# The scaled key of the RWKV units, turned by block transfers and VectorE in place of TensorE identity products

## The chip, the cores and the metric

One core of a Trainium2 chip runs the kernel. The metric is the device time of one execution in microseconds (us), as the median of the runs shown. The profile is of one execution.

## The reference

One layer of a decoder trunk is computed for a prompt of 1024 rows and for eight samples of eight rows (1088 rows in all), in fp32. What matters here is the RWKV branch, a state of 64x64 per head that each row updates:

```python
def wkv7_scan(state0, r, decay, k, v, kk, a):
    def step(S, inp):
        r_t, w_t, k_t, v_t, kk_t, a_t = inp
        sa = jnp.einsum("bhvk,bhk->bhv", S, -kk_t)
        S = (S * w_t[:, :, None, :]
             + sa[..., None] * (kk_t * a_t)[:, :, None, :]
             + v_t[..., None] * k_t[:, :, None, :])
        y = jnp.einsum("bhvk,bhk->bhv", S, r_t)
        return S, y
...
def trunk(x, c, shift0, pool0, wkv0, pos0, W):
...
        h = rms_norm(x, lp["norm_mix"]) * (1 + sc) + sh
        P = h @ lp["w_in"]
        pr, pp, pg = jnp.split(P, [RWKV_COLS, RWKV_COLS + POOL_WIDTH], axis=-1)
        o_r, s_shift, s_wkv, v_first = rwkv7_branch(pr, shift0[l], wkv0[l], v_first, lp)
        o_p, s_pool = pool_branch(pp, pool0[l], pos0, lp)
        g_r, g_p = jnp.split(jax.nn.sigmoid(pg), 2, axis=-1)
        merged = g_r * (o_r @ lp["w_br_rwkv"]) + g_p * (o_p @ lp["w_br_pool"])
        x = x + gt * (merged @ lp["w_out"])
...
        x = x + gt * (jnp.square(jax.nn.relu(h @ lp["w_ff1"])) @ lp["w_ff2"])
```

There are eight heads of 64 channels, and 1088 x 1024 rows go through the big products (`w_in`, `w_br`, `w_out`, `w_ff1`, `w_ff2`).

## The kernel before

Features lie on the partitions and rows in the free dimension. A fp32 weight is split into a high part (ScalarE, `whi`) and a low part (VectorE, `wlo`), and each big product is three matmuls (`mm3`): high by high, high by low, low by high.

There are two phases. In **phase 1** the big products of `w_in` and of half of `w_br` make one long **stream** on TensorE (jobs with `mm` banks; the last eight, `op_job`, multiply the pooling branch). Between the stream's matmuls stand the many small products of the RWKV branch. **Phase 2** follows with `or_job` (the RWKV half of `w_br`), `w_out` and the MLP; the first `or_job` needs the RWKV branch complete: its last quarter of the contraction reads the tile pair `hx` that `post(3)` writes.

The RWKV branch is worked off in four pairs of heads (`f` = 0 to 3), one after the other in `heads`. For each, `front` makes the scaled tensors and `scores` runs three **units**: u = 0 and u = 1 are the prompt's chunks 0 to 7 and 8 to 15 (a chunk is 64 rows), u = 2 the samples. In the order u = 0, 2, 1, each unit multiplies `bk` by `ra` and masks the result into `ab`, `at` and `ad` (VectorE and ScalarE). `ra` holds the scaled receptance in `[..., 0, :]` and the scaled, negated key in `[..., 1, :]`. Then `inverse`, `level`, `affine` and the serial `chain` (the state `S`, step by step) follow, and `post` normalizes and gates. In `affine`, `first` uses `at`, whose half `at[:, :, 0, :]` is the scaled key with rows and channels of each 64x64 block exchanged and the two heads' partition halves swapped. The prompt units of before get it by sixteen fp32 products with the identity into a PSUM bank `w`, which VectorE copies. The values `v` are turned in another way already: `swap` exchanges the 32x32 blocks of each 64x64 block by four transfers on SP's queue, from DRAM into `uv`, and VectorE transposes within the 32x32 blocks.

What sets the order: TensorE executes in the order in which a planner (`Clocks`, `Pace`) emits the program; it models when operands are ready and puts a small product between stream matmuls where it expects no wait. A request of `need` says for what a generator waits. The other engines' queues are put in order by a scheduler. All queues run in order. Everything is recorded through a helper, so most lines read L187 (VectorE, ScalarE, GpSimd, SyncE) or L358 (TensorE); rows are told apart by their tiles.

Of the kernel before, what the change touches and what calls it, by code (L numbers as in the profile page):

```python
# [9 lines left out]
F32 = mybir.dt.float32  # L10
# [8 lines left out]
P = 128  # L19
D = 1024  # L20
NPR = 1024
NSEQ = 8
TS = 8
NT = NPR + NSEQ * TS
# [297 lines left out]
class K:  # L322
# [565 lines left out]
    def ra(self, d, u):  # L888

        nc, kk, r, ev, es = self.nc, d["kk"], d["r"], d["ev"], d["es"]  # L890
        C = 8 if u < 2 else 1
        cs = slice(8 * u, 8 * u + C)
        ra = self.p1.tile([P, C, 2, 64], F32, tag=f"ra{C}", bufs=2 if u < 2 else 1, name=self.nm("ra"))
        d["qs"][u] = dict(ra=ra)
        if u < 2:
            nc.vector.scalar_tensor_tensor(ra[:, :, 1, :], cut(kk[:, :NPR])[:, cs], -1.0, ev[:, cs, 0:64], op0=ALU.mult, op1=ALU.mult)
            nc.vector.tensor_tensor(ra[:, :, 0, :], cut(r[:, :NPR])[:, cs], ev[:, cs, 1:65], op=ALU.mult)
        else:
            nc.vector.scalar_tensor_tensor(cut8(ra[:, 0, 1, :]), cut8(kk[:, NPR:NT]), -1.0, es[:, :, 0:8], op0=ALU.mult, op1=ALU.mult)
            nc.vector.tensor_tensor(cut8(ra[:, 0, 0, :]), cut8(r[:, NPR:NT]), es[:, :, 1:9], op=ALU.mult)  # L900
# [18 lines left out]
    def unit(self, f, d, u):  # L919
        nc = self.nc  # L920
        bk, end, v, ad, ao = (d[k] for k in ("bk", "end", "v", "ad", "ao"))
        ident = self.kc("ident")
        prompt = u < 2
        c0, C = 8 * u, 8 if prompt else 1
        cs = slice(c0, c0 + C)
        if u == 1 and f:
            yield lambda: ("c", f - 1, 1) in self.done
        if u:
            self.ra(d, u)
        tl = lambda tag, shape, n=2: self.p1.tile([P, C] + shape, F32, tag=f"{tag}{C}", bufs=n if prompt else 1, name=self.nm(tag))  # L930
        Q = dict(ab=tl("ab", [2, 128]), uv=tl("uv", [2, 64]), ra=d["qs"][u]["ra"])
        d["qs"][u] = Q
        ra, ab, uv = Q["ra"], Q["ab"], Q["uv"]
        if prompt:
            at = Q["at"] = tl("at", [2, 64])
            ak = at[:, :, 1, :]
            rest = [uv[hs, :, 1 - h, :] for h, hs in enumerate(HB)]
            for h, hs in enumerate(HB):
                self.swap(rest[h], cut(self.d_x[8 + f][hs, c0 * 64:(c0 + C) * 64]))
            strict, incl = self.kc("strict"), self.kc("incl")  # L940
        else:
            strict, incl = self.kc("strict8"), self.kc("incl8")
            ak = Q["ak"] = tl("ak", [64])
        for a in range(0, C, 4):
            m = min(4, C - a)
            us = slice(a, a + m)
            cu = slice(c0 + a, c0 + a + m)
            yield self.need(bk[:, cu], ra[:, us], banks=("w", "w"))
            pss = [self.ps("w") for _ in HB]
            for i in range(m):  # L950
                for hs, ps in zip(HB, pss):
                    self.mm(ps[:, i * 128:(i + 1) * 128], bk[hs, c0 + a + i, :, :].rearrange("p s j -> p (s j)"),
                            ra[hs, a + i, :, :].rearrange("p s j -> p (s j)"), start=True, stop=True)
            for h, (hs, ps) in enumerate(zip(HB, pss)):
                os = HB[1 - h]
                pv = ps[:, :m * 128].rearrange("p (c s j) -> p c s j", s=2, j=64)
                nc.vector.tensor_tensor(ab[:, us, h, 0:64], pv[:, :, 0, :], incl.unsqueeze(1).to_broadcast([P, m, 64]), op=ALU.mult)
                nc.vector.tensor_tensor(ak[hs, us, :], pv[hs, :, 1, :], strict[hs].unsqueeze(1).to_broadcast([64, m, 64]), op=ALU.mult)
                for b in range(2):
                    rq = slice(os.start + 32 * b, os.start + 32 * b + 32)  # L960
                    src = pv[rq, :, 1, 32 * b:32 * b + 32]
                    if prompt:
                        nc.scalar.activation(ad[rq, cu, :], src, AF.Copy)
                        if b == 0:
                            nc.scalar.activation(ao[rq, cu, :], pv[rq, :, 1, 32:64], AF.Copy)
                    else:
                        nc.vector.tensor_tensor(ad[rq, 16, :], src[:, 0, :], strict[rq, 32 * b:32 * b + 32], op=ALU.mult)
        bh = bk[:, cs, :, :].rearrange("p c s j -> p c (s j)")
        if prompt:
            nc.vector.tensor_tensor(bh, bh, end[:, cs].unsqueeze(2).to_broadcast([P, C, 128]), op=ALU.mult)  # L970
        else:
            for s in range(2):
                nc.vector.tensor_tensor(cut8(bk[:, 16, s, :]), cut8(bk[:, 16, s, :]), end[:, 16:24].unsqueeze(2).to_broadcast([P, 8, 8]), op=ALU.mult)

        if prompt:
            for h, hs in enumerate(HB):
                nc.vector.transpose(uv[hs, :, h, :], rest[h])
        yield self.need(ra, *[] if prompt else [v[:, NPR:NT]])
        ps = self.ps("w")
        for i in range(C):  # L980
            for h, hs in enumerate(HB):
                os = HB[1 - h]
                if prompt:
                    self.mm(ps[os, i * 64:(i + 1) * 64], ra[hs, i, 1, :], ident[hs, hs], start=True, stop=True, tile_position=(hs.start, os.start))
                else:
                    self.mm(ps[hs, 0:64], v[hs, NPR:NT], ident[hs, hs], start=True, stop=True)
        if prompt:
            nc.vector.tensor_copy(at[:, :, 0, :], cut(ps))
        else:
            for h, hs in enumerate(HB):  # L990
                nc.scalar.activation(uv[hs, 0, h, :], ps[hs, 0:64], AF.Copy)
        for a in range(0, C, 4):
            m = min(4, C - a)
            yield self.need(bh[:, a:a + m], wait=0, spare=900, slack=600)
            ps = self.ps("w")
            for i in range(m):
                self.tr(ps[:, i * 128:(i + 1) * 128], bh[:, a + i, :], ident)
            nc.scalar.activation(ab[:, a:a + m, :, 64:128], ps[:, :m * 128].rearrange("p (c h j) -> p c h j", h=2, j=64), AF.Copy)
        if prompt:
            yield self.need(ak, uv)  # L1000
            ps = self.ps("w")
            for i in range(C):
                for h, hs in enumerate(HB):
                    os = HB[1 - h]
                    self.mm(ps[os, i * 64:(i + 1) * 64], ak[hs, i, :], uv[hs, i, h, :], start=True, stop=True, tile_position=(hs.start, os.start))
            nc.scalar.activation(at[:, :, 1, :], cut(ps), AF.Copy)
# [90 lines left out]
    def affine(self, f, d):  # L1097
# [4 lines left out]
        def first(u):  # L1102
            Q = d["qs"][u]
            uv, at = Q["uv"], Q["at"]
            pss = [self.ps("w") for _ in range(2)]
            for i in range(8):
                for os in HB[::-1]:
                    self.mm(pss[i // 4][os, i % 4 * 128:(i % 4 + 1) * 128], z[os, 8 * u + i, :], at[os, i, :, :].rearrange("p s j -> p (s j)"),
                            start=True, stop=True)
            for a, ps in enumerate(pss):  # L1110
                us = slice(4 * a, 4 * a + 4)
                pv = ps.rearrange("p (c s j) -> p c s j", s=2, j=64)
                nc.scalar.activation(at[:, us, 0, :], pv[:, :, 0, :], AF.Copy)
                nc.vector.tensor_copy(uv[HB[1], us, 0, :], pv[HB[1], :, 1, :])
                nc.scalar.activation(uv[HB[0], us, 1, :], pv[HB[0], :, 1, :], AF.Copy)
# [972 lines left out]
def cut(t):  # L2088
    return t.rearrange("p (c j) -> p c j", j=64)
# [6 lines left out]
def cut8(t):  # L2096
    return t.rearrange("p (c j) -> p c j", j=8)


HB = (slice(0, 64), slice(64, 128))  # L2100
# [79 lines left out]
```

## Time and profile before

| | |
|---|---|
| time, median of 2 runs | 1602.77 us (1601.74 to 1603.8) |
| the profiled execution | 1604.23 us, its span 1602.4 us |
| TensorE (PE) busy | 1544.8 us, 96% of the span |
| VectorE (DVE) busy | 1097.8 us, 69% |
| ScalarE (ACT) busy | 662.7 us, 41% |
| DMA, mean | 181 GB/s, 37920 of 137438 packets under 512 B |

PE is a matmul's busy time, PEld its weight load, SPq the queue of transfers that SyncE issues. Times in a timeline are microseconds from the span's start; the first number of a row is its start, the second how long its group lasted. A bracket tells how long the engine was idle before and what released it. A fp32 matmul appears as two instructions, so sixteen products are 32 of them.

### The profile page before, as it was taken

Reading aid. Unit: us, or ns where it says so; the run is one execution under the profiler, and the core shown is the slowest. Engines: PE = TensorE matmul, PEld = TensorE weight load, DVE = VectorE, ACT = ScalarE, POOL = GpSimd, SP = SyncE. Lnnn points to the kernel's source line nnn. Section 1 sums busy time; section 2 is a strip of 40 time slices with the busy share of each in tenths; the row PEclk is TensorE's granted clock in tenths of the full one; section 3 lists DMA queues with packets and bytes.
Section 4 is the critical chain, followed back from the end, with each engine's and each line's share of the span. In section 5 each row is a group of like instructions: output and inputs, shape, how many; then the busy total and the mean of one; then the engine's idle time right before and its main releaser. Section 6 shows DMA issues by size and latency. Waiting matters only on the chain.

```text
span 1602.4 us, 34165 instructions
## 1 busy us (share of the span) xinstructions
PE 1544.8 (96%) x13851; PEld 1453.6 (91%) x13851; DVE 1097.8 (69%) x1932; ACT 662.7 (41%) x1286; POOL 139.1 (9%) x220
## 2 busy tenths in 40 slices
PE   4999999999998999999999999999999999999997
PEld 2898888988898879989998999999999999999997
DVE  4575758776876487547542697998767796666774
ACT  4454354455334544522222572222334344344651
POOL 0100100000000000012500120000000050000000
PEclk9999999999999999999999999999999999999999
DMA  9242523234333343855884555665345996664753
GB/s 343 89 134 76 181 84 112 93 127 133 101 122 104 113 125 106 322 180 186 310 295 162 183 198 170 237 212 200 139 151 213 387 365 196 213 200 142 234 192 119
DMA packets 137438, 290.32 MB, mean 181 GB/s; under 512 B 37920, under 2 KB 42016, under 8 KB 137280
## 3 DMA queue, kind: packets, MB, share of 16 engines
q1 hardware_dynamic: 129856, 266.75, 48.4%
q10 hardware_dynamic: 5360, 14.26, 2.6%
q0 software_dynamic: 2064, 7.13, 1.3%
q8 instruction: 109, 1.79, 0.5%
q14 instruction: 49, 0.40, 0.1%
HBM read 210.80 MB, written 77.28 MB: 180 GB/s over the span
## 4 chain that ended last, share of the span: by engine, by line
PE 76%; DVE 6%; DMA 4%; issue 2%; ACT 1%; SPq 1%; DVEq 0%; ACTq 0%
PE mm L358 50%; PE w L358 13%; PE wc L358 12%; DVE wt L187 1%; DVE hx L187 1%; DMA mg<-in_w_ff 1%; DMA wt<-d_x 1%; SPq L187 1%; DMA hid<-in_w_ada_mlp 1%; DVE wlo L187 1%; DMA hid<-in_w_ff 1%; PE w L389 0%; DVE hv L187 0%; ACT wt L187 0%; DMA uv<-d_x 0%
## 5 line engine op out<-in xcount | busy, mean ns | idle before, releaser
L358 PE MATMUL mm<-hx,whi 128*128 128x362 f32 (+2 forms) x2944 | 689.9, 322 | 6.4 <-ACT px L187 3.7
L358 PEld LDWEIGHTS mm<-hx,whi 128*128 128x128 f32 x2944 | 497.3, 190 | 29.2 <-issue 11.5
L358 PE MATMUL mm<-hx,wlo 128*128 128x362 f32 (+2 forms) x1472 | 463.7, 315 | 5.8 <-DVE wlo L187 5.8
L358 PEld LDWEIGHTS mm<-hx,wlo 128*128 128x128 f32 x1472 | 279.5, 190 | 6.6 <-DVE wlo L187 6.6
L358 PE MATMUL mm<-mg,whi 128*128 128x272 f32 (+2 forms) x1312 | 249.5, 289 | 0.5 <-DVE t L187 0.5
L358 PEld LDWEIGHTS mm<-mg,whi 128*128 128x128 f32 x1312 | 205.4, 188 | 5.1 <-issue 2.5
L358 PE MATMUL mm<-mg,wlo 128*128 128x272 f32 (+2 forms) x656 | 188.5, 287 | 0.0
L358 PE MATMUL wc<-hx,whi 128*128 128x272 f32 x896 | 170.4, 287 | 0.0
L358 PEld LDWEIGHTS wc<-hx,whi 128*128 128x128 f32 x896 | 140.3, 188 | 0.0
L187 ACT ACTIVATE whi<-hid 128x512 fp32r<-128x512 f32 x128 | 80.4, 630 | 144.6 <-PE mm L358 59.6
L358 PE MATMUL wc<-hx,wlo 128*128 128x272 f32 x448 | 128.9, 288 | 1.0 <-DVE wlo L187 1.0
L358 PEld LDWEIGHTS mm<-mg,wlo 128*128 128x128 f32 x656 | 123.5, 188 | 0.0
L187 DVE TENSOR_TENSOR wlo<-hid,whi 128x512 fp32r<-128x512 f32 x128 | 87.9, 688 | 48.5 <-ACT whi L187 47.9
L187 DVE TENSOR_TENSOR wlo<-wraw,whi 128x512 fp32r<-128x512 f32 x84 | 60.7, 724 | 68.1 <-ACT whi L187 64.6
L187 ACT ACTIVATE whi<-wraw 128x512 fp32r<-128x512 f32 x100 | 62.6, 627 | 94.0 <-PE mm L358 56.9
L358 PE MATMUL w<-hx,whi 128*128 128x272 f32 (+1 forms) x480 | 96.9, 296 | 0.0
L358 PEld LDWEIGHTS wc<-hx,wlo 128*128 128x128 f32 x448 | 84.2, 188 | 1.3 <-DVE wlo L187 1.2
L187 POOL TENSOR_TENSOR hx<-hx,rs 128x64 f32<-128x64 f32 x24 | 35.2, 1465 | 569.5 <-DMA mg<-in_w_ff 376.2
L358 PEld LDWEIGHTS mm<-mg,hx 128*128 128x128 f32 x576 | 72.9, 188 | 5.0 <-issue 5.0
L358 PEld LDWEIGHTS w<-hx,whi 128*128 128x128 f32 x480 | 77.0, 188 | 0.0
L358 PE MATMUL mm<-mg,hx 128*128 128x272 f32 (+2 forms) x576 | 75.5, 290 | 0.0
L187 ACT ACTIVATE px<-mm 128x362 f32<-128x362 f32 (+3 forms) x113 | 46.3, 435 | 60.7 <-PE mm L358 53.9
(275 smaller groups left out, 2312.7 us busy)
## 6 DMA issues: line engine op xcount, KB each, us to landing
t<-d_t SPq DMA_DIRECT2D x56, 544.0 KB, 4.9
hid<-in_w_ff SPq DMA_DIRECT2D x110, 256.0 KB, 3.8
d_t<-hx SPq DMA_DIRECT2D x102, 272.0 KB, 2.2
hid<-in_w_ff SPq DMA_DIRECT2D x42, 512.0 KB, 3.8
wraw<-in_w_in SPq DMA_DIRECT2D x68, 256.0 KB, 2.8
mg<-in_w_ff SPq DMA_DIRECT2D x58, 256.0 KB, 5.4
hid<-in_w_ada_mlp SPq DMA_DIRECT2D x24, 512.0 KB, 5.7
d_th<-px SPq DMA_DIRECT2D x22, 544.0 KB, 3.0
```

Of the source, the lines that this page charges most:

```text
L187: return f(*a, **kw)
L358: return self.nc.tensor.matmul(out, lhsT, rhs, **kw)
```

## The change

`ra` now also allocates the unit's tile `ab`, and as soon as the scaled key is made, `swap` asks for eight transfers (four for each head) that exchange its 32x32 blocks into `ab[..., 0, 64:128]`, a place that is free until the later turn of `bk` writes there. In the unit, VectorE then transposes within the 32x32 blocks from there into `at[:, :, 0, :]`. The sixteen identity products, their PSUM bank, VectorE's copy and the request (`need(ra)`) ahead of them are gone for the prompt's units; the samples' unit is as before.

```diff
@@ ra
         ra = self.p1.tile([P, C, 2, 64], F32, tag=f"ra{C}", bufs=2 if u < 2 else 1, name=self.nm("ra"))
-        d["qs"][u] = dict(ra=ra)
+        ab = self.p1.tile([P, C, 2, 128], F32, tag=f"ab{C}", bufs=2 if u < 2 else 1, name=self.nm("ab"))
+        d["qs"][u] = dict(ra=ra, ab=ab)
         if u < 2:
             nc.vector.scalar_tensor_tensor(ra[:, :, 1, :], cut(kk[:, :NPR])[:, cs], -1.0, ev[:, cs, 0:64], op0=ALU.mult, op1=ALU.mult)
+            for h, hs in enumerate(HB):
+                self.swap(ab[HB[1 - h], :, 0, 64:128], ra[hs, :, 1, :])
             nc.vector.tensor_tensor(ra[:, :, 0, :], cut(r[:, :NPR])[:, cs], ev[:, cs, 1:65], op=ALU.mult)
@@ unit
-        Q = dict(ab=tl("ab", [2, 128]), uv=tl("uv", [2, 64]), ra=d["qs"][u]["ra"])
-        d["qs"][u] = Q
+        Q = d["qs"][u]
+        Q["uv"] = tl("uv", [2, 64])
...
-        yield self.need(ra, *[] if prompt else [v[:, NPR:NT]])
-        ps = self.ps("w")
-        for i in range(C):
+        if prompt:
+            nc.vector.transpose(at[:, :, 0, :], ab[:, :, 0, 64:128])
+        else:
+            yield self.need(v[:, NPR:NT])
+            ps = self.ps("w")
             for h, hs in enumerate(HB):
-                os = HB[1 - h]
-                if prompt:
-                    self.mm(ps[os, i * 64:(i + 1) * 64], ra[hs, i, 1, :], ident[hs, hs], start=True, stop=True, tile_position=(hs.start, os.start))
-                else:
-                    self.mm(ps[hs, 0:64], v[hs, NPR:NT], ident[hs, hs], start=True, stop=True)
-        if prompt:
-            nc.vector.tensor_copy(at[:, :, 0, :], cut(ps))
-        else:
+                self.mm(ps[hs, 0:64], v[hs, NPR:NT], ident[hs, hs], start=True, stop=True)
             for h, hs in enumerate(HB):
                 nc.scalar.activation(uv[hs, 0, h, :], ps[hs, 0:64], AF.Copy)
```

Counted over the program, TensorE loses 128 products of 64x64, VectorE exchanges eight copies for eight transposes of 128x8x64, SP's queue gains 64 transfers of 32x8x32, and ScalarE has 17 loads of an activation table where it had 23. Since the planner places everything anew, the order of phase 1 changes on all engines; the order of phase 2 is the same.

The first place is VectorE in the front of the first pair of heads, between the first `ra` and the weights' low part that the stream needs next (`wlo_1120` before, `wlo_1127` now). Before:

```order
L187 SCALAR_TENSOR_TENSOR ds_1062<-px_925,part,d_1061 128x64
L187 STREAM_TRANSPOSE uv_1472<-uv_1472 64x8x64
L187 SCALAR_TENSOR_TENSOR ra_1468<-wt_697,e_1011 128x8x64
L187 TENSOR_TENSOR ra_1468<-wt_1009,e_1011 128x8x64
L187 SCALAR_TENSOR_TENSOR ra_1382<-wt_697,e_1011 128x64
L187 TENSOR_TENSOR ra_1382<-wt_1009,e_1011 128x64
L187 STREAM_TRANSPOSE uv_1472<-uv_1472 64x8x64
L187 TENSOR_TENSOR bk_1015<-wt_696,wt_901 64x9x64 x2
L187 SCALAR_TENSOR_TENSOR bk_1015<-wt_902,wt_901 64x9x64 x2
L187 TENSOR_TENSOR wlo_1120<-wraw_1117,whi_1119 128x512
```

The same place now:

```order
L187 SCALAR_TENSOR_TENSOR ds_1071<-px_925,part,d_1070 128x64
L187 SCALAR_TENSOR_TENSOR ra_1486<-wt_697,e_1011 128x8x64
L187 TENSOR_TENSOR ra_1486<-wt_1009,e_1011 128x8x64
L187 SCALAR_TENSOR_TENSOR ra_1422<-wt_697,e_1011 128x64
L187 TENSOR_TENSOR ra_1422<-wt_1009,e_1011 128x64
L187 STREAM_TRANSPOSE at_1236<-ab_1047 128x8x64
L187 TENSOR_TENSOR bk_1015<-wt_696,wt_901 64x9x64 x2
L187 SCALAR_TENSOR_TENSOR bk_1015<-wt_902,wt_901 64x9x64 x2
L187 TENSOR_TENSOR wlo_1127<-wraw_1124,whi_1126 128x512
```

Two transposes of `uv` and one more a few rows further up have moved behind `wlo`, and one new transpose of `ab` stands in their place.

The second place is VectorE in the last unit (u = 1) of the third pair of heads, behind `ra`. Before, the masks of the unit's products follow at once:

```order
L187 SCALAR_TENSOR_TENSOR ra_5017<-wt_4253,e_4457 128x8x64
L187 TENSOR_TENSOR ra_5017<-wt_4455,e_4457 128x8x64
L187 TENSOR_TENSOR ab_5020<-w_5052,kct 128x4x64
L187 TENSOR_TENSOR at_5022<-w_5052,kct 64x4x64
L187 TENSOR_TENSOR ab_5020<-w_5053,kct 128x4x64
```

Now the transpose of the exchanged blocks stands three rows behind `ra`, and the pooling branch's work (`d`, `psm`, `px`) lies around it:

```order
L187 SCALAR_TENSOR_TENSOR ra_5069<-wt_4317,e_4537 128x8x64
L187 TENSOR_TENSOR ra_5069<-wt_4535,e_4537 128x8x64
L187 TENSOR_TENSOR wlo_5124<-wraw_5121,whi_5123 128x512
L187 TENSOR_TENSOR d_5135<-px_4935 128x1038
L187 TENSOR_TENSOR psm_5136<-psm_4936 128x183
L187 STREAM_TRANSPOSE at_5082<-ab_5070 128x8x64
L187 TENSOR_TENSOR px_4934<-d_5135 128x1036
L187 TENSOR_TENSOR psm_5139<-psm_5136 128x181
L187 TENSOR_TENSOR ab_5070<-w_5177,kct 128x4x64
```

What moved: VectorE now waits in its queue for transfers that can only start once the row five places ahead is done.

The third place is TensorE at the end of phase 1. `post(3)` works in three pieces of the rows, each with two sums over a head (products `w<-wt,kct`: one of `y`, one of its square). Before, the very last of them stands inside the stream, with 66 stream matmuls (the rest of this `op_job` and the next) between it and the first `or_job`:

```order
L358 MATMUL mm_8260<-hx_7484,whi_8185 128x362
L358 MATMUL mm_8260<-hx_7486,whi_8185 128x362
L358 MATMUL mm_8260<-hx_7484,wlo_8186 128x362
L358 MATMUL w_8268<-wt_8144,kct 128x362
L358 MATMUL mm_8261<-hx_7484,whi_8185 128x362
L358 MATMUL mm_8261<-hx_7486,whi_8185 128x362
L358 MATMUL mm_8261<-hx_7484,wlo_8186 128x362
```

Now the last stream matmul of phase 1 (`mm_8208`) comes ahead of the last three sums, and the first `or_job` (`mm_8333`) directly behind them:

```order
L358 MATMUL mm_8208<-hx_7188,whi_8087 128x362
L358 MATMUL mm_8208<-hx_7190,whi_8087 128x362
L358 MATMUL mm_8208<-hx_7188,wlo_8088 128x362
L358 MATMUL w_8258<-wt_8184,kct 128x362
L358 MATMUL w_8267<-wt_7132,kct 128x362
L358 MATMUL w_8275<-wt_8184,kct 128x362
L358 MATMUL mm_8333<-hx_7192,whi_8304 128x364
```

VectorE's rows behind the middle one of these sums (`w_8267`, of the third piece's `y`) are now, up to the low half of `hx` that the first `or_job` reads in its last quarter:

```order
L187 SCALAR_TENSOR_TENSOR wt_7132<-w_8267,wt_7132 128x362
L187 RECIPROCAL wt_8184<-wt_8184 128x182
L187 RECIPROCAL wt_8184<-wt_8184 128x180
L187 TENSOR_TENSOR hx_8285<-wt_7132,hx_8284 128x364
L187 RECIPROCAL wt_8184<-wt_8184 128x182
L187 RECIPROCAL wt_8184<-wt_8184 128x180
L187 TENSOR_TENSOR wt_7132<-wt_7132,wt_8184 128x362 x2
L187 TENSOR_TENSOR wt_7132<-wt_7132,wt_8124 128x362 x2
L187 TENSOR_TENSOR wt_7132<-wt_7132,wt_8123 128x362 x2
L187 TENSOR_TENSOR hx_8285<-wt_7132,hx_8284 128x362 x2
```

What moved is the RWKV branch against the stream: by the stream matmuls ahead of it, its last sum stood at 2670 of phase 1's 2736 before, and stands at 2736 now.

## Prediction

> **What bounds the kernel now.** I read the page first:
>
> ```profile
> span 1602.4 us, 34165 instructions
> PE 1544.8 (96%) x13851; PEld 1453.6 (91%) x13851; DVE 1097.8 (69%) x1932; ACT 662.7 (41%) x1286; POOL 139.1 (9%) x220
> PE 76%; DVE 6%; DMA 4%; issue 2%; ACT 1%; SPq 1%; DVEq 0%; ACTq 0%
> ```
>
> TensorE is busy for 96% of the span and makes 76% of the chain that ended last, so a product taken from it should shorten the run wherever it runs without gaps. The change touches phase 1 alone, so I cut the span there (columns: stretch, then busy time of each engine, last the granted clock, DMA share and rate):
>
> ```profile
> 60.00:740.00 680.00, 657.34 (x6984) 593.43 (x6984) 459.83 (x839) 305.47 (x636) 50.53 (x136) 0.98 0.40 131
> 740.00:1602.00 862.00, 850.63 (x6672) 835.75 (x6670) 601.91 (x1042) 328.51 (x613) 85.74 (x69) 1.00 0.62 216
> ```
>
> Phase 1 leaves TensorE idle for 680.0 - 657.3 = 22.7 us. The list of waits in that stretch says for whom:
>
> ```profile
> PE wc L358 <- DVE S L187: 6.4, 5, 2.8
> PE mm L358 <- ACT px L187: 3.7, 3, 3.1
> PE mm L358 <- DVE wlo L187: 3.4, 1, 3.4
> ```
>
> Three single waits (2.8, 3.1 and 3.4 us) are 9.3 of it. An idle stretch has a second price, the clock behind it:
>
> ```profile
> 124.29 0.67 PE L358 MATMUL mm<-hx,wlo 128*128 128x364 f32 x1 [3.37 <-DVE wlo L187]
> 124.30:131.20 6.90, 6.90 (x33) 6.28 (x34) 5.90 (x9) 2.50 (x7) 0.77 (x2) 0.55 0.67 216
> 402.72 0.33 PE L358 MATMUL wc<-S,ra 64*64 64x64 f32 x4 [1.15 <-DVE S L187]
> 404.00:407.50 3.50, 3.50 (x20) 2.10 (x21) 3.47 (x6) 1.46 (x3) 1.26 (x2) 0.57 0.27 93
> ```
>
> After 3.37 us of idling the clock stood at 0.55 for 6.9 us, which costs 0.45 x 6.9 = 3.1 us more; after 1.15 us it stood at 0.57 for 3.5 us, 1.5 us more.
>
> **The change part by part.** *The identity products.* One group of sixteen in the timeline of TensorE:
>
> ```profile
> 138.69 0.33 PE L358 MATMUL mm<-hx,wlo 128*128 128x364 f32 x1
> 138.95 1.15 PE L358 MATMUL w<-kct,ra 64*64 64x64 f32 x32
> 140.03 0.60 PE L358 MATMUL mm<-hx,whi 128*128 128x362 f32 x2
> ```
>
> From the start of the stream matmul ahead to that of the one behind are 1.34 us; two stream matmuls follow each other at 0.165 us (27 of them take 4.46 us in rows below). So a group costs the stream 1.34 - 0.165 = 1.17 us, its two changes of tile shape included. Eight units lose one each: **8 x 1.17 = 9.4 us** less for TensorE. By the group's busy time alone it is 9.2:
>
> ```profile
> L358 PE MATMUL w<-kct,ra 64*64 64x64 f32 x256 | 9.2, 221 | 0.0
> L187 DVE COPY at<-w 128x512 f32<-128x512 f32 x8 | 5.5, 692 | 4.5 <-PE w L358 4.4
> L187 DVE STREAM_TRANSPOSE uv<-uv 64x512 f32<-64x512 f32 x16 | 11.3, 704 | 9.0 <-DMA uv<-d_x 8.8
> L187 DVE STREAM_TRANSPOSE iv<-iv 128x512 f32<-128x512 f32 x16 | 16.2, 1048 | 0.0
> L187 SPq DMA_DIRECT2D uv<-d_x x64: 303/448/1882, 104.0 to 575.3; - x64
> uv<-d_x SPq DMA_DIRECT2D x64, 32.0 KB, 2.3
> ```
>
> *VectorE's transpose* of 128x8x64 isn't in this trace. It lies between the copy (0.69 us) that it replaces and the strided `iv` transposes (1.05 us): 0 to 0.36 us more, eight times, at most 2.9 us on an engine that is busy 460 of 680 us here. I take the contiguous `uv` transpose (0.70 us), and so nothing.
>
> *The transfers.* Each unit adds eight to SP's queue. From SBUF to SBUF there is no row; the same blocks from DRAM are issued in 0.45 us and land 2.3 us later. So a unit's blocks are there 8 x 0.45 + 2.3 = 5.9 us after the key, and SP issues 64 x 0.45 = 29 us more in 680, mostly while it would wait. By the extremes of that row (0.30 and 1.88 us each) it is 4.7 to 17 us; I take the median, as 64 such transfers made it.
>
> *A new wait.* Five of the eight units have 10 or more instructions' time between the key and VectorE's transpose. In the three units u = 1 of the later heads the transpose follows soon. In the second place shown of the order, three rows lie between:
>
> ```profile
> 479.70 1.25 DVE L187 TENSOR_TENSOR d<-px 128x1032 f32<-128x1032 f32 x1
> 480.84 0.37 DVE L187 TENSOR_TENSOR psm<-psm 128x177 f32<-128x177 f32 x1
> 123.55 0.69 DVE L187 TENSOR_TENSOR wlo<-wraw,whi 128x512 fp32r<-128x512 f32 x1
> ```
>
> These are 1.25 + 0.37 + 0.69 = 2.3 us, so VectorE waits some 5.9 - 2.3 = 3.6 us there; in the other two (masks, a transpose of 1.05 us and a `wlo` between) some 2.5 us. Queued behind are `wlo` of the stream's next weights and the masks that free the `w` banks; TensorE waits for both. What reaches it has no row: between nothing, where the weights are ahead, and all of it with a slow clock, 3.6 + 2 x 2.5 + 3 x 3.1 = 18 us. The `uv` transposes, which waited for transfers six times (8.8 us), stand near one wait of TensorE for `wlo`, 3.4 us; at that rate three new waits cost 3/6 x 3.4 = **1.7 us**, which I take.
>
> *VectorE's order at the first front* (the first place). The `wlo` at 123.55 us was the one that TensorE waited 3.37 us for. Three `uv` transposes that stood ahead of it are behind it now and one new one is ahead, so it comes 2 x 0.70 = **1.4 us** earlier. The exchange of this unit starts some 12 us before its transpose and is hidden. Without that cover the gain is 0.
>
> *The end of phase 1* (the third place). The freed time comes out only if the RWKV branch is done by the end of the stream. Before:
>
> ```profile
> 724.37 1.38 PE L358 MATMUL w<-wt,kct 128*128 128x362 f32 x4
> 725.78 0.54 DVE L187 SCALAR_TENSOR_TENSOR wt<-w,wt 128x362 f32<-128x362 f32 x1
> 726.35 0.51 ACT L187 ACTIVATE wt<-wt 128x362 f32<-128x362 f32 x1
> 731.54 0.77 PE L358 MATMUL w<-wt,kct 128*128 128x362 f32 x2
> 732.35 0.56 ACT L187 ACTIVATE wt<-w,eps 128x362 f32<-128x362 f32 x1 [1.09 <-PE w L358]
> 733.62 2.41 DVE L187 RECIPROCAL wt<-wt 128x182 f32<-128x182 f32 x2
> 736.35 0.52 DVE L187 TENSOR_TENSOR wt<-wt,wt 128x362 f32<-128x362 f32 x1
> 736.90 0.69 ACT L187 ACTIVATE wt<-wt,part 128x362 f32<-128x362 f32 x1 [2.66 <-DVE wt L187]
> 740.25 0.54 DVE L187 TENSOR_TENSOR hx<-wt,hx 128x362 fp32r<-128x362 f32 x1 [0.57 <-ACT hx L187]
> 743.06 0.50 PE L358 MATMUL mm<-hx,whi 128*128 128x364 f32 x2
> 747.52 0.50 PE L358 MATMUL mm<-hx,whi 128*128 128x364 f32 x2
> ```
>
> The last sum starts at 731.54, `hx` is complete at 740.79, and the first `or_job` (from 743.06) reads it at 747.52: 6.7 us to spare. In the new order nothing of the stream lies behind the last sums. Let the last three of them start at t. The third piece's `y` is summed at t+1.4, VectorE subtracts (0.54) and ScalarE squares (0.51), so the last sum starts at t+2.6: TensorE idles **1.2 us**. It ends at t+3.4, and the `or_job` runs its first 27 matmuls to t+7.9 and the first three of its last quarter, whose `hx` is done, to t+8.4. VectorE has from t+2.05 two reciprocals (2 x 2.41), a product for `hx` (0.54), six products (0.52 each) with ScalarE's scaling (0.69) and copy (0.51) between: by these durations and with some 0.1 us a handover `hx` is there, middle piece first, at t+11.3 and t+11.9. TensorE idles 2.9 and, with half a microsecond of the middle piece done by then, 0.1 us: **4.2 us** in all. With the eleven handovers free it is 3.1, at 0.2 us each 5.3.
>
> Two idle stretches of 1.2 and 2.9 us lie 5 us apart. By the trace, 1.15 us brought 1.5 us of slow clock once, but the waits of 0.8 to 1.1 us elsewhere brought none; 3.4 us brought 3.1. I take **1.6 us** between nothing and 3.1. The Trainium skill (TensorE: Matmul & The Clock Gate, "Why this matters for your kernels") asks only that no idle gap exceed about 3 us; by that rule this term is 0, and the sum 1.6 us lower. The row at 402.72 disagrees: there a gap of 1.15 us was enough.
>
> *The sum.* -9.4 + 4.2 + 1.6 + 1.7 - 1.4 = **-3.3 us**. Against the profiled execution, 1604.23 us, that is 1600.9. This execution lies 1.46 us above the median shown, 1602.77, so the median I expect is 1602.77 - 3.3 = **1599.5** us.
>
> **The rivals.**
>
> *All of it comes through.* VectorE's waits cost nothing and the end of phase 1 is covered. Then it is -9.4 - 1.4 = -10.8, 1592 us; if the replanning also drops one of the three long waits (3.1 us idle and 3.1 of clock), 1586. For it speaks that ScalarE loses six table loads; against it the order at the end of phase 1, where no cover is left. Chance 0.2.
>
> *VectorE's new waits decide: slower than before.* If all three reach TensorE with the slow clock, 18 us take the place of 1.7: -3.3 + 16.3 = +13.0, 1616 us; if two do, about 1610. The place is the transpose of `ab` at u = 1, the price 2.5 to 3.6 us of idling and 3.1 of clock each; it decides from the point where the stalled `wlo` is the next weight that TensorE loads, and beats the gain from the second such wait. For it speaks that the blocks can't land before 5.9 us; against it that a stream weight lasts TensorE 36 x 0.165 = 5.9 us and is split one weight ahead. Chance 0.22.
>
> *The change does nothing.* The RWKV branch is paced by its serial steps on VectorE, and TensorE idles at the end of phase 1 for all that it saves: 1602.8. The planner's later place for the branch speaks for it; that TensorE's order is fixed and dense speaks against it. Chance 0.13, inside my range.
>
> **How the numbers follow.** The forecast, with the waits of phase 1 dealt anew but of the same sum, give or take 4 us (1596 to 1604), has 0.45. The low end reaches into the first rival, the high end to two stalls that reach TensorE: 1590 to 1611. A difference of 2% (32 us), about what a measurement of this kernel can tell from no change, is out of reach of every case worked out: within 2% 0.97, faster 0.01, slower 0.02 for a stalled queue that I don't see.
>
> **What would show it.** In the profile after, `w<-kct,ra` must be gone and the eight transposes of `at` be near 0.70 us. At the end of phase 1, TensorE must show waits of about 1.2 and 2.9 us ahead of `w<-wt,kct` and of `mm<-hx`; if there are none, that term is wrong. The wait for `wlo` near 124 us must be about 2 us. VectorE must wait for transfers from `ra` to `ab` three times; if TensorE shows waits for `wlo` or `ab` right behind, the slower rival holds. The forecast fails if SP's queue is held up by the 64 transfers, so that weights come late, or if the transfers land much later than 2.3 us.

## The result, and the profile after

The changed kernel takes **1629.3 us** (median of 2 runs, 1628.06 to 1630.56) where the kernel before takes 1602.8: the ratio is 1.0164, 95% interval 1.0138 to 1.019. It is slower by 26 us; the forecast was 1599.5, the upper end of the range 1611.

The page of the changed kernel:

```profile
span 1628.7 us, 33745 instructions
PE 1546.1 (95%) x13595; PEld 1453.8 (89%) x13595; DVE 1100.3 (68%) x1932; ACT 653.9 (40%) x1280; POOL 139.6 (9%) x220
PE 73%; DVE 9%; DMA 4%; issue 2%; ACT 2%; SPq 1%; POOL 0%; DVEq 0%; ACTq 0%; POOLq 0%
```

The 256 instructions of the identity products are gone from TensorE, but its busy time is 1.3 us longer, and VectorE has 9% of the chain that ended last where it had 6%. Span less busy time is TensorE's idle time: 1628.7 - 1546.1 = 82.6 us, before 1602.4 - 1544.8 = 57.6. So the 26.3 us of the two spans are **25.0 of idling and 1.3 of busy time**, and since by the prediction's estimate 9.4 us of work left, the busy time holds some 1.3 + 9.4 = 10.7 us of slower clock. The same stretches as before (phase 1 ends later now, so the second one is longer):

```profile
60.00:740.00 680.00, 636.67 (x6574) 576.07 (x6572) 442.22 (x803) 287.61 (x610) 48.64 (x133) 0.96 0.40 131
740.00:1628.00 888.00, 872.58 (x6837) 852.91 (x6833) 621.53 (x1076) 337.66 (x631) 88.14 (x72) 0.99 0.61 212
```

TensorE idles 43.3 us in the first 680 where it idled 22.7, at a clock of 0.96 where it had 0.98. The list of its waits over the whole span says for what (first row: the waits for "issue" of the kernel before; its waits for `S` stand in the prediction):

```profile
PE w L358 <- issue: 1.7, 2, 0.9
PE w L358 <- issue: 18.9, 2, 17.3
PE wc L358 <- DVE S L187: 11.0, 7, 5.0
PE w L358 <- ACT wt L187: 4.7, 7, 2.1
PE mm L358 <- DVE wlo L187: 3.1, 2, 1.8
PE mm L358 <- DVE px L187: 2.5, 1, 2.5
```

One wait of 17.3 us is new, and the waits for the state `S` grew from 6.4 to 11.0 us. The list gives the long one to "issue", that is to nothing it can see. The timelines of TensorE (first row) and of VectorE around that place name it:

```profile
440.08 2.76 PE L358 MATMUL w<-px,plw 128*128 128x364 f32 x4 [17.35 <-issue]
436.88 1.23 DVE L187 SCALAR_TENSOR_TENSOR px<-d,px 128x1024 f32<-128x1024 f32 x1
438.02 0.70 DVE L187 STREAM_TRANSPOSE at<-ab 128x512 f32<-128x512 f32 x1
438.65 1.25 DVE L187 TENSOR_TENSOR wt<-wt,wt 128x1088 fp32r<-128x1088 f32 x1
439.82 0.16 DVE L187 COPY px<-zf 128x7 f32<-128x7 f32 x1
422.00:440.00 18.00, 0.73 (x5) 0.43 (x3) 17.78 (x30) 3.17 (x5) 1.81 (x3) 0.60 0.25 62
440.00:447.00 7.00, 6.92 (x77) 5.41 (x79) 1.19 (x2) 1.12 (x2) 0.00 (x0) 0.56 0.28 82
```

The waiting product is not of the RWKV units at all. It is the third pooling group's (`pools`), which reads `px`; VectorE ends `px` with a copy at 439.82 + 0.16 = 439.98, and TensorE starts 0.1 us later. No row of VectorE around it waits: it works 17.78 of the 18 us (the last two rows are the windows with busy time by engine). The front of the next pair of heads stands in its queue between the steps of the pooling branch. TensorE's order is fixed ahead of time, so everything of the stream behind that product waits too, and the 7 us after it run at 0.56 of the clock.

The three places that the prediction speaks of, on TensorE (the first front, the last sums, the first `or_job`), and VectorE's transposes at u = 1, with the price of the new operations:

```profile
123.22 0.43 PE L358 MATMUL mm<-hx,wlo 128*128 128x364 f32 x1 [1.28 <-DVE wlo L187]
765.01 0.88 PE L358 MATMUL w<-wt,kct 128*128 128x362 f32 x2 [2.11 <-ACT wt L187]
772.78 1.00 PE L358 MATMUL mm<-hx,whi 128*128 128x362 f32 x2 [1.93 <-ACT hx L187]
297.92 0.71 DVE L187 STREAM_TRANSPOSE at<-ab 128x512 f32<-128x512 f32 x1 [1.88 <-DMA ab<-ra]
488.66 0.71 DVE L187 STREAM_TRANSPOSE at<-ab 128x512 f32<-128x512 f32 x1 [0.47 <-DMA ab<-ra]
648.23 0.71 DVE L187 STREAM_TRANSPOSE at<-ab 128x512 f32<-128x512 f32 x1 [2.05 <-DMA ab<-ra]
L187 DVE STREAM_TRANSPOSE at<-ab x8: 694/707/712, 118.8 to 648.2; 128x512 f32<-128x512 f32 x8
L187 SPq DMA_DIRECT2D ab<-ra x64: 586/608/2221, 107.9 to 646.1; - x64
```

All three waits for blocks are there, shorter than forecast, and so is the idling at the end of phase 1. They are not the main part of what made the kernel slower; the experiments say what did.

### The profile page after: what moved, and what is told of

It is laid out like the page before. It is cut to its first block, busy times and chain, and to the rows that moved or that the text cites. A ratio compares the mean times of both kernels' runs of the same rounds, so it can differ in the third digit from the quotient of the medians.

```text
span 1628.7 us, 33745 instructions
## 1 busy us (share of the span) xinstructions
PE 1546.1 (95%) x13595; PEld 1453.8 (89%) x13595; DVE 1100.3 (68%) x1932; ACT 653.9 (40%) x1280; POOL 139.6 (9%) x220
## 4 chain that ended last, share of the span: by engine, by line
PE 73%; DVE 9%; DMA 4%; issue 2%; ACT 2%; SPq 1%; POOL 0%; DVEq 0%; ACTq 0%; POOLq 0%
PE mm L358 49%; PE wc L358 13%; PE w L358 11%; DVE wt L187 2%; SPq L187 1%; DVE hv L187 1%; DMA mg<-in_w_ff 1%; DVE bk L187 1%; DVE wlo L187 1%; DMA hid<-in_w_ada_mlp 1%; DVE hx L187 1%; DVE mg L187 0%; DMA wraw<-in_w_br 0%; PE w L389 0%; DMA wt<-d_x 0%
```

## The experiments

Theory A: the planner, dealing the order anew, put a pooling product ahead of what VectorE can deliver. Theory B: the transfers and VectorE's waits for them cost the time. Theory C: the lost cover at the end of phase 1 does. (Theory D, which one expectation below names already, is taken up with e5.) Results first, as ratios to the kernel before on the same chip (95% interval), with TensorE's busy and idle time in the profiled execution (kernel before: 1544.8 and 57.6 us):

| run | median, us | ratio | busy | idle |
|---|---|---|---|---|
| changed kernel | 1629.3 | 1.0164 (1.0138 to 1.019) | 1546.1 | 82.6 |
| e4, no transfers | 1629.5 | 1.016 (1.0128 to 1.0193) | 1542.2 | 86.1 |
| e1a, product later | 1625.1 | 1.0121 (1.0087 to 1.0155) | 1549.8 | 77.3 |
| e1b, product far later | 1617.3 | 1.0074 (1.005 to 1.0098) | 1545.6 | 71.3 |
| e7, all pooling later | 1637.2 | 1.0204 (1.0189 to 1.0219) | 1551.5 | 85.1 |
| e2b, planner not told | 1603.1 | 1.0002 (0.9989 to 1.0015) | 1544.3 | 62.3 |
| e2, old order | 1603.7 | 0.9994 (0.9974 to 1.0014) | 1539.0 | 68.0 |
| e5, old order, no transfers | 1595.6 | 0.9952 (0.9938 to 0.9967) | 1531.1 | 60.2 |
| e11, as e5, transfers unread | 1601.1 | 0.9988 (0.9976 to 0.9999) | 1535.5 | 63.8 |
| e12, the same by GpSimd | 1599.1 | 0.9978 (0.9965 to 0.999) | 1534.7 | 61.1 |
| e3, before plus transfers | 1607.9 | 1.0024 (1.0013 to 1.0035) | 1544.6 | 61.4 |
| e8, as e2, by GpSimd | 1602.1 | 0.999 (0.9976 to 1.0004) | 1536.7 | 65.0 |
| e9, as e2, by ScalarE | 1607.2 | 1.0028 (1.0013 to 1.0043) | 1542.6 | 69.4 |
| e10, as e2, behind `uv` | 1601.3 | 0.998 (0.9967 to 0.9993) | 1532.7 | 65.6 |
| e13, behind `uv`, two queues | 1598.2 | 0.9963 (0.9946 to 0.998) | 1535.7 | 61.9 |

The medians come from several chips, so runs are compared by their ratios. A profiled execution need not lie at its run's median: those of e2, e2b and e9 took 5 to 7 us more, that of e5 2.5 us less, so small differences in the last two columns are a hint and no more.

### Is it the transfers? (e4)

```diff
-                self.swap(ab[HB[1 - h], :, 0, 64:128], ra[hs, :, 1, :])
+                self.swap(ab[HB[1 - h], :, 0, 64:128], ra[hs, :, 1, :], False)
-            nc.vector.transpose(at[:, :, 0, :], ab[:, :, 0, 64:128])
+            nc.vector.transpose(at[:, :, 0, :], ra[:, :, 1, :])
```

With `False` the planner counts the transfer as in the changed kernel and none is asked for.

> The changed kernel with TensorE's order kept row for row, but the 64 transfers are left out: VectorE transposes the scaled key where it lies, so the four 32x32 blocks of a 64x64 block are not exchanged (this part of the result is left out). Theory A: the 17.35 us wait stays, since it is made by the order; 1625 to 1629 us, at most 4.4 us less for the three waits of VectorE for blocks. Theory B: without transfers the loss is gone, 1593 to 1600 us. Theory C: 1625 to 1629 us as well.

Measured: 1629.5 us, ratio 1.016, the changed kernel's. The timeline of TensorE still has the wait:

```profile
438.47 2.76 PE L358 MATMUL w<-px,plw 128*128 128x364 f32 x4 [17.33 <-issue]
```

Theory B falls for the changed kernel: without one transfer the same product waits 17.33 us. The three waits of VectorE, 4.4 us in all, leave no mark on the time; but the intervals reach some 0.3%, 5 us, to each side, so a part of them could hide there.

### Is it where the pooling product stands? (e1a, e1b, e7)

```diff
-                yield self.need(z[:, c0:c0 + m], plw, zs, wait=0, spare=6000)
+                yield self.need(z[:, c0:c0 + m], plw, zs, wait=0, spare=15000 if g == 2 else 6000)
```

e1b has 28000 in the same place; e7 has 25000 for all four groups. Expected of e1a, e1b and e7, in this order:

> The changed kernel, with one margin in the planner raised (15 instead of 6 us) for the third pooling group alone. Its products stand 27 stream matmuls and one step of the state chain (two groups of 16 small products) further back in TensorE's order; VectorE's order hardly moves. Theory A (the planner put these products ahead of what VectorE can deliver, and TensorE waits in order): 27 x 0.165 = 4.5 us and some 2 us of small products now fill the start of the 17.35 us wait, so 10 to 11 us of it are left and the run takes about 6.5 us less than the changed kernel, some 1623 us. Theory B (the 64 transfers and VectorE's waits for them are what the change costs): no difference, about 1629 us. Theory C (the loss of cover at the end of phase 1): no difference, since that part of the order is the same.

> The same margin at 28 us: the third pooling group's products stand 102 stream matmuls (16.8 us) and some 3 us of small products further back, past the place where VectorE finishes them. Theory A: the 17.35 us wait is gone, and the slow clock behind it (7 us at 0.56, 3.1 us) with it: 17.35 + 3.1 = 20 us less than the changed kernel, 1609 us; what is left above the kernel before is in the smaller waits. Theory B: 1629 us. Theory C: 1629 us, as the end of phase 1 keeps its order.

> The changed kernel with the planner's margin for all four pooling groups at 25 instead of 6 us. The third group's products stand at stream matmul 1608 (changed kernel 1503), and the RWKV branch comes out earlier: its last unit at 2199 instead of 2397 of the stream, near the 2217 of the kernel before. Theory A: the 17.35 us wait is gone (20 us with its slow clock) and the 4 us at the end of phase 1 too, 1604 to 1608 us. Theory B: 1625 to 1629 us. Theory D adds that it comes no lower than the kernel before, 1602.

Measured by the ratios: e1a 0.43% or 6.9 us less than the changed kernel (theory A: 6.5), e1b 0.9% or 14 us less (theory A: 20), e7 0.4% more (theory A: 21 to 25 us less). Only e1b's interval lies clear of the changed kernel's; e1a's overlaps it and e7's touches it, so for these two it is the traces that speak. TensorE's timelines of e1a (two rows) and e1b (one row) at the place:

```profile
429.56 1.98 PE L358 MATMUL wc<-ab,uv 128*64 128x64 f32 x32 [4.47 <-DVE S L187]
439.95 2.79 PE L358 MATMUL w<-px,plw 128*128 128x364 f32 x4 [3.39 <-DVE px L187]
430.68 1.97 PE L358 MATMUL wc<-ab,uv 128*64 128x64 f32 x32 [4.46 <-DVE S L187]
```

In e1a the wait for the pooling product is down from 17.35 to 3.39 us and named, `px` of VectorE. But the state chain's products, which now come first, wait 4.47 us for `S`, whose update stands in the same unbroken stretch of VectorE's work. In e1b only that one is left at this place: 17.35 - 4.46 = 12.9 us of idling gone, which is what my 20 overlooked (over the whole span it is 82.6 - 71.3 = 11.3). That theory A holds for the long wait is shown: the product was moved, hardly anything else (18 of VectorE's 1932 rows in e1a, 26 in e1b), and the wait went. As e1b keeps TensorE's order at the end of phase 1, theory C is not the main cause. What e1b still has above the kernel before, 0.74% or 12 us, no run takes apart. The list of TensorE's waits in e7:

```profile
PE wc L358 <- DVE S L187: 11.8, 7, 4.9
PE w L358 <- DVE d L187: 6.0, 5, 2.3
PE mm L358 <- DVE wlo L187: 5.9, 4, 1.8
PE w L358 <- issue: 5.6, 4, 2.2
```

The long wait and the idling at the end of phase 1 are both gone there, and a crowd of waits of 1 to 5 us costs more than both (85.1 us idle), with 6.7 us more busy time than before for 9.4 us less work. So this margin is no cure: it deals the order anew once more, and here no better.

### The change without its re-dealt order (e2, e2b)

In e2 the planner goes on counting the identity products, their bank and the copy, but none is issued (`dry`), and the transfers and the transpose are hidden from it (`hush`); TensorE's rows are those of the kernel before, less the 256. In e2b the planner is told of neither the products nor the transfers. Where TensorE's order is held, as in e2 and later in e3, the scheduler still places the other engines' rows anew: of VectorE's 1932 rows, 100 stand elsewhere in e2 than in the kernel before, and 36 in e3. The two expectations, of e2 and of e2b:

```diff
+            yield self.need(ra)
+            ps = self.ps("w")
+            self.dry = True
...
+            self.dry = False
+            on = self.hush()
             nc.vector.transpose(at[:, :, 0, :], ab[:, :, 0, 64:128])
+            self.clocks.on = on
```

> The whole change, with its real transfers and VectorE transposes, but the planner is told nothing of them: it goes on counting the sixteen identity products, their bank and the copy, so TensorE's order is that of the kernel before, row for row, without the 256 products. Theory A (the re-planned order is the cost): the 17.35 us wait does not arise, the end of phase 1 keeps its 6.7 us of cover, and the removed 9.4 us come through, with 1.4 us from the earlier weight split near 124 us and up to 1.7 us of new waits: 1602.8 - 9 = 1592 to 1596 us. Theory B: the 64 transfers and the waits for them are still there, so it is slower than the kernel before, 1615 to 1629 us. Theory C: about 1594 us too, because the cover is back; e1b tells C from A.

> The whole change, with transfers; the planner sees neither the identity products nor the transfers nor VectorE's transpose, so it plans anew with 9.4 us less of TensorE's work and no dependence on the transfers. The pooling products stand where they stood before (third group at stream matmul 1545 to 1551, before 1542 to 1545), the last unit at 2229 (before 2217, changed kernel 2397). Theory A (the changed kernel lost by where its planner put things, the planner having counted a wait of the masks for the transfers): about as fast as the kernel before or a little faster, 1596 to 1605 us. If the transfers themselves were the cost: 1615 us or more.

Measured: 1603.7 and 1603.1 us, both no different from the kernel before. The loss is gone in both, with all transfers issued and read, so the re-dealt order made it; and where the planner is told of nothing (e2b), its own deal comes out near the old one, so it was what it counted for the tile, the transfers and the transpose that turned the order. (By the code, it compares extents, so that masks into `ab[..., 0:64]` count as waiting for blocks that land in `ab[..., 64:128]`. That this is the step in it was not tried.) But theory A wanted 1592 to 1596 for e2, and that gain did not come either (e2b lies inside its 1596 to 1605). In e2, VectorE (first row) and TensorE near 250 us:

```profile
250.56 0.71 DVE L187 STREAM_TRANSPOSE at<-ab 128x512 f32<-128x512 f32 x1 [1.55 <-DMA ab<-ra]
254.01 0.43 PE L361 MATMUL wc<-S,ra 64*64 64x64 f32 x4 [3.22 <-DVE S L187]
```

VectorE waits 1.55 us for blocks in a stretch of dense work, and the state's update, four rows further back, makes TensorE wait 3.22 us, before 0.98.

### Where the gain went in the old order (e5, e11, e12, e3)

Theory B2: VectorE's waits for blocks ate it. Theory D: the products were never on the path. Theory F: the issues on SP's queue delay the `uv` blocks behind them. Theory G: the traffic itself. e5 is e2 with VectorE's transpose reading `ra` and no transfers; e11 is e5 with the transfers, which nothing reads; e12 has them asked for by GpSimd; e3 is the kernel before with transfers that nothing reads.

```diff
-            nc.vector.transpose(at[:, :, 0, :], ab[:, :, 0, 64:128])
+            nc.vector.transpose(at[:, :, 0, :], ra[:, :, 1, :])
```

The expectations of e5, e3, e11 and e12:

> As the run with the old order (TensorE's order of the kernel before, without the 256 identity products), but without the 64 transfers: VectorE transposes the scaled key where it lies, so the 32x32 blocks are not exchanged (this part of the result is left out). The old order with transfers gave 1603.7, the same as before, though TensorE had 9.4 us less to do, and VectorE waited 7.8 us for blocks in four places. Theory B2 (those waits ate the gain): without transfers they are gone, and the run takes 1593 to 1597 us. Theory D (the products were not on the path: what stands behind them in TensorE's order waits for VectorE and ScalarE, so TensorE only comes earlier to its waits): no difference from the run with transfers, 1601 to 1604 us, and the waits for S, px, bk and hv stay.

> The kernel before, row for row on TensorE and with its identity products and copies, plus the 64 transfers into ab, which nothing reads. It prices the transfers alone: 64 issues of 0.61 us on SP's queue and their traffic, with no engine waiting for them but a later ScalarE copy into the same place. Theories A and D: no difference, 1603 to 1606 us. Theory F (the transfers hold up SP's queue, so that weights and keys of the stream come late): 1608 us or more, with TensorE waits for wlo or for whi that the kernel before does not have.

> The old order with the 64 transfers on SP as soon as the key is made, but VectorE transposes the scaled key where it lies and reads nothing of them (the exchange of blocks is left out of the result). Theory F (their 39 us of issue time on SP's queue delay the uv blocks and weights): little less than with the blocks read, 1600 to 1604 us. Theory B2 (VectorE's waits for the blocks are the cost): 1595 to 1597 us, as without transfers.

> The same, with the unread transfers asked for by GpSimd; VectorE's order is that of the run without transfers but for one row. What is left is their traffic and GpSimd's time. Theory F: 1595 to 1597 us, as without transfers. Theory G (the traffic of 16384 packets of 128 B itself delays the other transfers, or GpSimd's work that others wait for): 1600 us or more.

Measured: e5 0.9952, 7.7 us less than before (interval 5 to 10), so D falls. That is the edit without its transfers as a whole: the products are gone, the wait for `wlo` near 124 us is shorter as well (2.29 us for 3.37), and 95 of VectorE's rows stand elsewhere.

With unread transfers on SP's queue (e11) 5.8 us of that are gone, and the two intervals do not meet; theory F had 1600 to 1604 for it. But in e11 the scheduler has also moved 22 of VectorE's rows against e5, transposes of `uv` among them, and other transfers in SP's queue, so the 5.8 us are the price of the transfers together with what they displace. e12 is the cleaner run, with SP's order as in e5 and one row of VectorE moved: 4.2 us are gone, the intervals touch, and 1599.1 lies between theory F's 1597 and theory G's 1600. That the blocks are read as well (e2 against e11) makes no difference that can be told. So the transfers cost by being there, not by being waited for: B2 falls as the main term.

e3 agrees, 0.24% slower (0.13 to 0.35) with no product removed, though its 1607.9 lies between the two ranges of its expectation, and TensorE's waits for `wlo` did not grow as theory F had it. One place where the cost arises can be read from the trace. SP's queue of the kernel before (first row) and of e3 (three rows), then e3's VectorE, ScalarE and TensorE:

```profile
409.41 3.77 SPq L187 DMA_DIRECT2D uv<-d_x  x8
409.23 5.63 SPq L187 DMA_DIRECT2D ab<-ra  x8
414.96 1.53 SPq L187 DMA_DIRECT2D uv<-d_x  x3
417.04 2.41 SPq L187 DMA_DIRECT2D uv<-d_x  x5
419.97 0.70 DVE L187 STREAM_TRANSPOSE uv<-uv 64x512 f32<-64x512 f32 x1 [2.61 <-DMA uv<-d_x]
425.66 0.27 ACT L187 ACTIVATE iv<-w 32x128 f32<-32x128 f32 x1 [5.62 <-DVE at L187]
426.42 0.49 PE L358 MATMUL w<-ra,bk 64*128 64x128 f32 x2 [1.96 <-ACT iv L187]
```

Eight issues of the scaled key stand 5.63 us ahead of the unit's `uv`, which is asked for 6.3 us later at its end (419.45 against 413.18). VectorE, which did not wait there before, waits 2.61 us; the masks behind come late, ScalarE waits 5.62 us for them (2.88 before), and TensorE waits 1.96 us for a bank, which it did not before. That is theory F in one place. It is not all: e12 leaves SP's queue as it was and still stands 0.26% above e5 by the medians. How issue time and traffic divide the rest stays open.

### Other queues (e8, e9, e10, e13)

All four are e2 with its transfers read; what changes is who asks for them and when.

```diff
@@ ra (e2)
-                self.swap(ab[HB[1 - h], :, 0, 64:128], ra[hs, :, 1, :])
@@ ra (e8; "scalar" in e9)
+                self.swap(ab[HB[1 - h], :, 0, 64:128], ra[hs, :, 1, :], "gpsimd")
@@ unit, behind the swaps of uv (e10)
+                self.swap(ab[HB[1 - h], :, 0, 64:128], ra[hs, :, 1, :])
@@ unit, behind the swaps of uv (e13)
+                self.swap(ab[HB[1 - h], :, 0, 64:128], ra[hs, :, 1, :], ("sync", "gpsimd")[h])
```

The expectations of e8, e9, e10 and e13:

> The whole change in the old order (TensorE's rows as in the run with the old order), but the 64 transfers are asked for by GpSimd, which is busy for 9% of the span, instead of SP. Theory F (the 64 issues of 0.61 us stand in SP's queue ahead of the uv transfers of the same unit, so VectorE's uv transposes and the masks behind them come late): with SP's queue free of them most of the 8 us between the old order with transfers (1603.7) and without (1595.6) comes back, 1595 to 1599 us, and VectorE's waits for uv go back to about 9 us. Theory B2 (VectorE's own waits for the blocks, 7.8 us, are the cost): the blocks still land no sooner, so 1602 to 1605 us. If GpSimd's issues are much slower than SP's, the waits for blocks grow and it is slower than before.

> The same with the 64 transfers asked for by ScalarE (40% busy). Theory F: SP's queue is free, but ScalarE now spends its time on the issues, in the stretch where it also splits weights and frees the w banks: between 1596 and 1604 us, by how long an issue holds it. Theory B2: 1602 to 1605 us.

> The whole change in the old order, with the 64 transfers on SP, but each unit's eight are asked for behind its eight uv transfers, not as soon as the key is made. VectorE's order stays but for 14 rows. Theory F: the uv blocks come as early as in the kernel before, and the scaled key's blocks, which are read last of the unit's transposes, come 4.9 us after them; VectorE waits for those instead in the units whose transposes follow at once. Net 1598 to 1604 us, with the uv waits back to about 9 us and the ab waits above 7.8 us. Theory B2 (the ab waits are the cost): slower than the old order with early requests, 1604 to 1608 us.

> The whole change in the old order, the eight transfers of a unit asked for behind its uv transfers, four by SP and four by GpSimd. Theory F: SP's extra issue time is halved and the blocks land 2.4 us after uv's instead of 4.9: 1597 to 1600 us, faster than the kernel before by 0.3%. Theory G: as with all on SP behind uv, 1601 us.

Measured: e8 1602.1 (theory F wanted 1595 to 1599: missed), e9 1607.2 (missed, above the 1604 allowed), e10 1601.3 and e13 1598.2 (both inside theory F's ranges). VectorE's waits for these transfers in e2 (two rows) and in e8 (one row), then ScalarE and TensorE in e9 and its issues, then the issues and landing of e13:

```profile
DVE uv L187 <- DMA uv<-d_x: 9.8, 8, 2.1
DVE at L187 <- DMA ab<-ra: 7.8, 4, 2.5
DVE uv L187 <- DMA uv<-d_x: 7.9, 5, 2.3
115.41 0.63 ACT L187 ACTIVATE whi<-wraw 128x512 fp32r<-128x512 f32 x1 [7.79 <-DMA ab<-ra]
116.46 0.97 PE L361 MATMUL mm<-hx,whi 128*128 128x362 f32 x2 [6.29 <-ACT px L187]
L187 ACTq DMA_DIRECT2D ab<-ra x64: 592/622/1077, 107.3 to 617.2; - x64
L187 POOL DMA_DIRECT2D ab<-ra x32: 584/584/615, 107.4 to 601.6; - x32
L187 SPq DMA_DIRECT2D ab<-ra x32: 586/607/1541, 110.2 to 601.4; - x32
DMA to landing us min/median/max: 1.8/2.4/5.7
```

In e8 what theory F asks for came: VectorE waits 7.9 us for `uv` and for no block any more. The gain did not come, so freeing SP's queue is not enough; why is open. In e9 ScalarE does nothing else for 7.79 us while eight requests pass through its queue, and TensorE waits 6.29 us for its copy of `px` (this is the slowest of e9's twelve executions). **By the medians e13 is the fastest version that does the whole change, and it beats both kernels: it is 0.37% (0.2 to 0.54%) below the kernel before**, as the best of four tried; e10 is 0.2% below it (0.07 to 0.33%). "As soon as it is made" was the worse moment on SP's queue by the medians (e2 1603.7, e10 1601.3), though the intervals of e2, e10 and e13 meet. The Trainium skill (DMA: Bandwidth & Descriptors, "Issuing engines are not separate DMA queues") says that asking from several engines saves only the sequencers' time to initiate, usually small against the transfer. Here that time is no small part: eight issues of 0.61 us are 4.9 us against a landing of 1.9 us.

## Why the prediction was wrong

**The step that failed** is the one behind the sum: "with the waits of phase 1 dealt anew but of the same sum, give or take 4 us". The 26.3 us between the spans are -9.4 of work, 25.0 of idling and 10.7 of slower clock. Without the end of phase 1 (4.0 and 1.7, below) the waits that I put at the same sum came to 21.0 us more idling and some 9.0 of slower clock; what VectorE's new waits and the first front did is contained in that. 17.35 is one pooling product; the waits for `S` gave 11.0 - 6.4 = 4.6 more. I read the order at three places that the diff pointed to, and took TensorE's order to be dense everywhere else. It is only dense if VectorE, whose own order was dealt anew as well, keeps up. The third pooling group's products had moved forward, to 1503 matmuls of the `mm` banks ahead of them from 1542, while the RWKV branch's front moved back, onto the pooling branch in VectorE's queue; both stood in the orders that I had, at none of my three places.

**The slow clock**, 1.6 us, was meant for the two idle stretches at the end of phase 1, and there it was right: behind the second the clock stood at 0.50 for 3.4 us (first row below), 1.7 us more. The other 9.0 us are elsewhere, 3.1 of them behind the pooling product (7 us at 0.56), and go with the step above, but for up to 3.4 us near 33 and 57 us, where the clock stood at a half although TensorE's order is still that of before. By the rule that no idle gap should exceed about 3 us (the Trainium skill, TensorE: Matmul & The Clock Gate, "Why this matters for your kernels") the term would have been nothing; this trace disagrees, as gaps of 1.93 us there and of 1.52 and 1.34 us elsewhere had half clock behind them. The length of a gap does not decide alone either: one of 1.62 us had none (last two rows).

```profile
773.80:777.20 3.40, 3.40 (x13) 3.40 (x13) 0.77 (x3) 0.41 (x1) 1.30 (x1) 0.50 0.88 308
195.87 0.82 PE L358 MATMUL w<-iv,hv 32*32 32x32 f32 x73 [1.52 <-issue]
363.23 0.88 PE L358 MATMUL w<-wt,sw 128*128 128x362 f32 x2 [1.34 <-ACT wt L187]
197.00:203.50 6.50, 6.50 (x83) 5.23 (x76) 0.45 (x1) 3.53 (x6) 0.54 (x1) 0.50 0.65 218
364.20:367.50 3.30, 3.30 (x70) 2.85 (x68) 0.00 (x0) 0.66 (x2) 0.00 (x0) 0.50 0.57 177
231.03 0.33 PE L358 MATMUL wc<-S,ra 64*64 64x64 f32 x4 [1.62 <-DVE S L187]
231.00:237.00 6.00, 5.97 (x49) 5.60 (x50) 5.34 (x7) 2.13 (x5) 0.32 (x1) 1.00 0.13 44
```

**The identity products**, -9.4 us: in keeping with e5, which keeps the order and adds no transfers (-7.7, interval 5 to 10), though e5 has the shorter wait for `wlo` in it too, so that 9.4 lies at the upper end. **VectorE's transpose**, nothing: right, 0.707 us for 0.70.

**The transfers**, nothing beyond the waits for them: wrong. The issue took 0.61 us and not 0.45, the landing 1.9 and not 2.3, so eight blocks need 6.8 us and not 5.9; and 39 us of issue time on SP's queue, which I put "mostly while it would wait", delay what stands behind them. In the old order their presence costs 5.8 us on SP's queue (e11 against e5, with the rows that moved) and 4.2 on GpSimd's (e12). With 5.8 in place of nothing, the forecast of -3.3 us would have been +2.5.

**The new wait at u = 1**, 3.6 + 2.5 + 2.5 us on VectorE of which 1.7 reach TensorE: the places were right, the waits were 1.88, 0.47 and 2.05 us, and e4 shows no part of them in the time of the changed kernel, within some 5 us. The rival "VectorE's new waits decide" had the right sign and the wrong mechanism.

**VectorE's order at the first front**, -1.4 us: right in sign, the wait for `wlo` went from 3.37 to 1.28 us, 2.1 less, and to 2.08 us in the old order (e2). **The end of phase 1**, +4.2 us: right in sum, 2.11 + 1.93 = 4.0, with 0.9 more at the first wait than I had and 1.0 less at the second. In the changed kernel it is the smaller part of the loss, as read from the trace, for no run takes it alone; e2 and e2b, which keep the cover, do not have it.

## What to carry to other kernels

Where a planner deals the order anew, price every product on the in-order engine against the queue of the engine that feeds it, not only the products of the edit: the costly one here belonged to another branch. To learn what an edit itself is worth, keep the old order and take the edit alone; here that showed 7.7 us for the edit without its transfers, and most of it lost again with them. A transfer that is asked for early is not free: in an in-order queue it stands ahead of others that may be needed sooner.

## What the runs showed of the hardware that I had not expected

In the clock records of these traces the granted clock is 1 or a half, and the stretches at a half are multiples of 3.41 us (3.41, 6.83, 10.24, 13.65 and 20.48), but for the last of each trace; they also stand behind idle gaps of 1.34 and 1.52 us, and not behind one of 1.62. A small SBUF-to-SBUF transfer costs the asking engine about the same from three of them: 0.61 us on SP, 0.58 on GpSimd, 0.62 on ScalarE (medians of 64). And 64 transfers that nothing reads cost 4 to 6 us of 1600 where TensorE's order was held (e3, e11, e12; rows of VectorE moved with them in the first two).
